# Normalised tiles handed to the next layer as two 16-bit planes in DRAM and turned by transposing DMAs

## The chip, the cores and the metric

The kernel runs on one core of one Trainium2 chip. The metric is the device time of one execution in microseconds. A core has TensorE (PE in the profile, with its weight loads as PEld), VectorE (DVE), ScalarE (ACT), GpSimd (POOL) and SyncE (SP). SP issues the DMAs here, in program order, and 16 DMA engines carry them out.

## The reference

A sequence of 2048 tokens with 1024 features goes through four layers in float32. Each layer projects its input to several streams, mixes them by its own recurrences, attentions and gates, and projects the result back to 1024 features. Cut to the frame that the change touches:

```python
x = first_block(x, ...)     # layer 1: gated recurrence + sliding-window attention
x = second_block(x, ...)    # layer 2 (even) and layer 3 (odd), same frame
return third_block(x, ...)  # layer 4: y = rms_norm(x, norm_g); x + out_proj(...)

# the frame of layers 1 to 3
h = jnp.einsum('btd,de->bte', x, w_in)          # input projection, 1024 -> several thousand
mix = ...                                       # recurrences, attention, gates
out = jnp.einsum('bte,ed->btd', mix, w_out)     # output projection, 1024 -> 1024
z = ALPHA * x + out
x = (z - mean(z)) * rsqrt(var(z) + 1e-5) * ln_g + ln_b
```

So the normalised rows of one layer are needed twice by the next: with features on partitions, as the input of the projection, and with tokens on partitions, as the residual. Layer 4 needs them scaled by `norm_g` per feature.

## The kernel before, in words

**Tiling.** The tokens are cut into four blocks of 512 (`TB`). A step is one layer on one block. `run` takes the blocks in pairs and the layers within a pair: (layer 1, block 0), (1, 1), (2, 0), (2, 1), and so on to layer 4, then blocks 2 and 3. There are 16 steps. What a step leaves is used by the next layer two steps later.

**Matrix products.** Every product of the two projections is done in three: the input is split into `ah` (rounded to the fast 32-bit form) and `al` (what rounding lost), the weights into `hi` and `lo`, and TensorE adds `hi*ah`, `hi*al` and `lo*ah` in one PSUM bank. `ah` and `al` are single tiles of 128 features x 8 chunks x 512 tokens. `out_proj` uses the same two tiles for the mixed streams, so the next step's input can be written into them only piece by piece, as the last products of the step before have read them.

**Weights.** A weight piece is 1 MB in a tile of the pool `whl` with four buffers. On first use it is fetched, split by ACT (L458) and DVE (L315), and saved to DRAM (`wdr`); afterwards it is loaded whole by one DMA on SP (L452). SP waits until TensorE has left a buffer before it can issue the next piece.

**End of a step.** `out_proj` multiplies in two halves of 512 output columns. In the second half it takes tokens 0 to 255 first and tokens 256 to 511 after them, and normalises each tile of 128 tokens as it comes out: tiles 1 and 3 get scale and shift (`lng`, `lnb`) on DVE at once, tiles 0 and 2 are only centred and scaled by their deviation on ACT. What remains is put into `pending` as four calls of `tail`, one for a tile of 128 tokens, and for layer 3 a fifth, `rms_row`.

**`tail`.** It turns a tile of 128 tokens x 1024 features by eight transposes on TensorE (`tr`, L327, each 128x128) into two PSUM banks. ACT copies them out to two tiles of the pool `t`: for tiles 0 and 2 in pieces of 128 with the scale and shift per feature (L707), for tiles 1 and 3 in one copy (L699), in layer 3 with the scale `ng`. Two DMAs (L708) write them to `chn` in DRAM, which then holds the features on partitions. For tiles 0 and 2 DVE then applies scale and shift to the rows, and one DMA (L714) writes the rows to `rows`.

**Start of a step.** All layers begin with `in_b4`: four groups of 128 output columns, each with its own weight piece and PSUM bank, first over tokens 0 to 255 (24 matmuls of 128x256 a group), then over tokens 256 to 511. After the first three groups of the first pass, and after the first two of the second, `flush` takes one call from `pending`. The `tail` of the step before thus runs inside the first products of the next.

**`load_x`.** For a new step it calls `load_x1` eight times, for each tile of 128 tokens and each half of the features: one DMA of 256 KB from `chn` (for layer 1 from the input `xt`, which lies in DRAM already turned) to a tile of the pool `u`, ACT's cast to `ah` (L587) and DVE's subtraction to `al`.

**Order.** The order of the instructions on each engine, and of the DMAs on SP, comes from a planner that runs when the kernel is built. It goes by the order in which the program states them, by tile buffers that come free and by priorities (`hp` for weights and some evictions). On the chip each engine keeps its order and waits on semaphores. Pools bound how far it runs ahead: 13 buffers of `u`, 7 of `t`, 4 of `whl`; four of `u` hold `lng` and `lnb` until the last `tail`.

Of the kernel before, what the change touches and what calls it, by code (L numbers as in the profile page):

```python
# [10 lines left out]
F32 = mybir.dt.float32  # L11
F32R = mybir.dt.float32r
I32 = mybir.dt.int32
U8 = mybir.dt.uint8
BF16 = mybir.dt.bfloat16
AF = mybir.ActivationFunctionType
ALU = mybir.AluOpType
# [3 lines left out]
D = 1024  # L21
T = 2048
TB = 512
# [203 lines left out]
class Build:  # L227
# [114 lines left out]
    def setup(self):  # L342
        nc = self.nc
# [14 lines left out]
        nc.gpsimd.affine_select(out=cm, in_=ones[:, 0:128], compare_op=ALU.is_ge, fill=0.0, base=0, pattern=[[1, 128]], channel_multiplier=-1)  # L358
        self.cmask = self.const([128, 128], U8, "cmask")
        nc.vector.tensor_copy(self.cmask, cm)  # L360
# [3 lines left out]
        nc.gpsimd.affine_select(out=self.amask, in_=zero, compare_op=ALU.is_ge, fill=NEGB, base=0, pattern=[[1, 128]], channel_multiplier=-1)  # L364
        self.rst = self.const([128, 512], BF16, "rst")
        nc.vector.memset(self.rst, 1.0)
# [10 lines left out]
        self.chn, self.rows = {}, {}  # L377
        for l in self.layers[:-1]:
            for i in range(2):
                self.chn[l, i] = self.dp.tile([4, 128, D], F32, tag=f"chn{l}{i}", name="chn")  # L380
                self.rows[l, i] = self.dp.tile([4, 128, D], F32, tag=f"rows{l}{i}", name="rows")

        lb = self.const([128, 4], F32, "lb")
# [15 lines left out]
        for n in ("hgw", "glag", "retg", "pscale", "mlg"):  # L399
            h = self.const([128, 4], F32, n + "h")  # L400
# [155 lines left out]

    def load_x(self, b, l):
        if not self.start:
            for t in range(4):
                for i in range(2):  # L560
                    self.load_x1(b, l, t, i)
            return

        ws = []
        self.wi, self.wpos = "wi1", 0
        for parts in (((0, 0), (1, 0)), ((0, 1), (1, 1)), ((2, 0), (3, 0)), ((2, 1), (3, 1))):
            for t, i in parts:
                with self.hp():
                    self.load_x1(b, l, t, i)
            ws.append(self.next_w())  # L570
        self.ahead, self.start = ws, False
        self.lc = self.lconst(l, b)
        with self.later(300):
            self.save()
# [5 lines left out]
    def load_x1(self, b, l, t, i):  # L580
        nc = self.nc
        st = self.u()
        src = self.I["xt"][b] if l == 1 else self.chn[l - 1, b % 2]
        self.first(nc.sync.dma_start(st, src[t, :, i * 512:i * 512 + 512]))
        c = slice(t * 128, t * 128 + 128)
        h = self.ah[:, 4 * i:4 * i + 4, c]
        nc.scalar.copy(h, c4(st))  # L587
        self.tt(self.al[:, 4 * i:4 * i + 4, c], c4(st), h.bitcast(F32), ALU.subtract)

    def load_xr(self, b, l):  # L590
        self.xr = self.big(self.at, [128, 4, D], F32)
        src = self.I["xr"][b] if l == 1 else self.rows[l - 1, b % 2]
        for t in range(4):
            self.tc.keep_in_program_order(self.nc.sync.dma_start(self.xr[:, t], src[t]))
# [93 lines left out]
    def tail(self, layer, b, xr, t, lng, lnb):  # L688

        nc = self.nc  # L690
        x = xr[:, t]
        for j in range(2):
            ps = self.mm()
            for i in range(4):
                k = 4 * j + i
                self.tr(ps[:, i * 128:i * 128 + 128], x[:, k * 128:k * 128 + 128])
            f = self.t()
            if t % 2 and layer < 3:
                nc.scalar.copy(f, ps)  # L699
            else:  # L700
                for i in range(4):
                    o = slice(i * 128, i * 128 + 128)
                    if t % 2:
                        self.act(f[:, o], ps[:, o], AF.Copy, scale=self.col("ng", 4 * j + i))
                    else:
                        k = 8 * (layer - 1) + 4 * j + i
                        self.act(f[:, o], ps[:, o], AF.Identity, scale=self.lgn[:, k:k + 1], bias=self.lbn[:, k:k + 1])  # L707
            nc.sync.dma_start(self.chn[layer, b % 2][t, :, j * 512:j * 512 + 512], f)  # L708
        if t % 2 == 0:
            for i in range(2):  # L710
                xi = x[:, i * 512:i * 512 + 512]
                self.tt(xi, xi, lng[i], ALU.mult)
                self.tt(xi, xi, lnb[i], ALU.add)
        nc.sync.dma_start(self.rows[layer, b % 2][t], x)  # L714

    def rms_row(self, b, xr):
# [1096 lines left out]
def c4(ap):  # L1813
    return ap.rearrange("p (a b) -> p a b", a=4)
# [22 lines left out]
```

## Time and profile before

| | |
|---|---|
| time, median of 3 runs | 3685.34 us (3682.23 to 3688.99) |
| the profiled execution | 3691.55 us, span 3689.8 us |
| TensorE busy | 3652.1 us (99%) in 20576 matmuls |
| VectorE busy | 2256.2 us (61%) |
| ScalarE busy | 1389.5 us (38%) |
| GpSimd busy | 14.9 us |
| DMA | 798.03 MB, 60.6% of 16 engines' span |
| granted TensorE clock | 0.999 |
| DMAs from `chn` (L584) | 96 of 256 KB, median 7.0 us to landing |
| DMAs to `chn` (L708) | 96 of 256 KB, median 3.5 us to landing |

Busy times are those of the records, and records of neighbouring matmuls overlap: the busy time of a group is what it adds to the engine's cover, the mean is the length of one record. In a row of groups the columns are line, engine, operation, what is written from what is read, shapes and count, then busy us and mean ns, then the idle time before it and who ended that. In a timeline row they are start, length, engine, line, operation, tiles and count.

### The profile page before, as it was taken

The numbers are of one execution on the slowest core, as the hardware profiler recorded it, in microseconds if no ns is written. First come the engines' busy times: TensorE is split into PE (matmuls) and PEld (weight loads), VectorE is DVE, ScalarE is ACT, GpSimd is POOL, SyncE is SP. The second block draws the span as 40 slices with busy tenths as digits, with TensorE's granted clock in tenths as the row PEclk, the third lists the DMA queues.
The fourth block names the chain that finished last, engine by engine and source line by source line (L and its number), as shares of the span: only waits on it lengthen the run. The fifth ranks groups of instructions, "written<-read, shape, count | busy, mean of one in ns | idle before, by whom it ended". The sixth has DMA issues, their size and how long they took to land.

```text
span 3689.8 us, 53341 instructions
## 1 busy us (share of the span) xinstructions
PE 3652.1 (99%) x20576; PEld 3090.4 (84%) x20576; DVE 2256.2 (61%) x5796; ACT 1389.5 (38%) x2890; POOL 14.9 (0%) x37
## 2 busy tenths in 40 slices
PE   8999999999999999999999999999999999999999
PEld 7888888888787888888888888989887878888887
DVE  7765566555755598587556556444454546883874
ACT  6636343323341355235254372313121313541451
POOL 0000000000000000000000000000000000000000
PEclk9999999999999999999999999999999999999999
DMA  7784577856885784853644645657475747446534
GB/s 274 252 291 156 199 266 278 296 182 231 308 305 202 249 288 166 296 189 104 215 180 167 251 167 185 241 178 267 161 259 182 275 176 254 149 145 208 184 114 160
DMA packets 161823, 798.03 MB, mean 216 GB/s; under 512 B 17952, under 2 KB 18080, under 8 KB 93984
## 3 DMA queue, kind: packets, MB, share of 16 engines
q1 hardware_dynamic: 161568, 794.62, 60.6%
q8 instruction: 162, 2.65, 0.3%
q14 instruction: 93, 0.76, 0.1%
HBM read 593.02 MB, written 201.52 MB: 215 GB/s over the span
## 4 chain that ended last, share of the span: by engine, by line
PE 60%; DVE 3%; ACT 1%; issue 0%; DMA 0%; SPq 0%; POOL 0%; POOLq 0%; DVEq 0%; ACTq 0%
PE acc L324 50%; PE mm L324 7%; PE mm L327 3%; DVE u L312 1%; DVE t L315 0%; DVE whl L315 0%; DVE big L312 0%; ACT t L302 0%; ACT u L301 0%; ACT t L301 0%; DMA wst<-in_wi_dram 0%; ACT whl L458 0%; DVE ss L1437 0%; ACT big L301 0%; DMA chn<-t 0%
## 5 line engine op out<-in xcount | busy, mean ns | idle before, releaser
L324 PE MATMUL acc<-whl,ah 128*128 128x512 f32 (+3 forms) x6144 | 1815.2, 379 | 2.8 <-DVE mix L312 1.9
L324 PEld LDWEIGHTS acc<-whl,ah 128*128 128x128 f32 x6144 | 1111.7, 188 | 226.2 <-issue 4.8
L324 PE MATMUL acc<-whl,al 128*128 128x512 f32 (+3 forms) x3072 | 1159.0, 377 | 0.0
L324 PE MATMUL acc<-ah,whl 128*128 128x256 f32 (+1 forms) x4096 | 1062.4, 343 | 9.1 <-ACT whl L458 8.3
L324 PEld LDWEIGHTS acc<-ah,whl 128*128 128x128 f32 x4096 | 699.4, 189 | 92.2 <-ACT whl L458 8.5
L324 PE MATMUL acc<-al,whl 128*128 128x512 f32 (+1 forms) x2048 | 697.1, 340 | 0.0
L324 PEld LDWEIGHTS acc<-whl,al 128*128 128x128 f32 x3072 | 578.2, 188 | 114.4
L324 PEld LDWEIGHTS acc<-al,whl 128*128 128x128 f32 x2048 | 386.7, 189 | 40.0 <-issue 3.6
L315 DVE TENSOR_TENSOR whl<-wst,whl 128x1024 fp32r<-128x1024 f32 (+3 forms) x141 | 167.0, 1185 | 112.2 <-ACT whl L458 109.6
L458 ACT CAST whl<-wst 128x1024 fp32r<-128x1024 f32 (+3 forms) x141 | 143.4, 1019 | 169.2 <-PE acc L324 102.2
L587 ACT CAST ah<-u 128x512 fp32r<-128x512 f32 x128 | 78.4, 620 | 271.5 <-PE acc L324 249.2
L312 DVE SCALAR_TENSOR_TENSOR big<-big,acc 128x512 f32<-128x512 f32 x128 | 86.3, 680 | 134.9 <-PE acc L324 134.6
L312 DVE SCALAR_TENSOR_TENSOR u<-mix,hdw,u 128x512 f32<-128x512 f32 x240 | 166.2, 741 | 0.3
L312 DVE SCALAR_TENSOR_TENSOR g<-g,acc 128x512 f32<-128x512 f32 x80 | 55.0, 687 | 162.3 <-ACT g L301 162.0
L301 ACT ACTIVATE g<-acc 128x512 f32<-128x512 f32 x72 | 42.9, 597 | 236.6 <-PE acc L324 236.5
L315 DVE TENSOR_TENSOR al<-u,ah 128x512 fp32r<-128x512 f32 x128 | 86.7, 680 | 51.5 <-ACT ah L587 51.4
L301 ACT ACTIVATE t<-mm,cols 128x128 f32<-128x128 f32 (+2 forms) x272 | 98.3, 462 | 51.2 <-PE mm L327 48.5
L324 PE MATMUL mm<-big,u 128*128 128x256 f32 (+2 forms) x616 | 92.4, 285 | 1.3 <-DVE u L315 1.3
L324 PEld LDWEIGHTS mm<-big,u 128*128 128x128 f32 x616 | 83.8, 189 | 6.7 <-DVE u L315 1.5
L1020 DVE CUSTOM_DVE_ANT_0 t<-mm,lc,nsk 128x256 f32<-128x256 f32 (+1 forms) x128 | 55.0, 472 | 49.4 <-PE mm L324 49.1
L324 PEld LDWEIGHTS mm<-vb,t 128*128 128x128 f32 (+1 forms) x640 | 67.9, 169 | 16.1 <-issue 9.5
L324 PE MATMUL mm<-vb,t 128*64 128x128 f32 (+2 forms) x640 | 78.8, 278 | 1.6 <-DVE t L312 0.9
(338 smaller groups left out, 4062.3 us busy)
## 6 DMA issues: line engine op xcount, KB each, us to landing
whl<-wdr SPq DMA_DIRECT2D x396, 1024.0 KB, 4.8
wdr<-whl SPq DMA_DIRECT2D x132, 1024.0 KB, 4.9
wst<-in_wi_dram SPq DMA_DIRECT2D x99, 512.0 KB, 6.2
rows<-big SPq DMA_DIRECT2D x48, 512.0 KB, 4.7
chn<-t SPq DMA_DIRECT2D x96, 256.0 KB, 3.5
u<-chn SPq DMA_DIRECT2D x96, 256.0 KB, 7.0
big<-rows SPq DMA_DIRECT2D x48, 512.0 KB, 7.0
wst<-in_wo_dram SPq DMA_DIRECT2D x32, 512.0 KB, 5.7
```

The source lines that it names most:

```text
L301: return self.nc.scalar.activation(out, in_, f, bias=bias, scale=scale)
L312: return self.nc.vector.scalar_tensor_tensor(out, in0, s, in1, op0, op1)
L315: return (eng or self.nc.vector).tensor_tensor(out, a, b, op)
L324: return self.nc.tensor.matmul(out, lhsT, rhs, start=start, stop=stop)
L327: return self.nc.tensor.transpose(out, in_, self.ident)
L458: nc.scalar.copy(hi[:, c], st[:, c])
L587: nc.scalar.copy(h, c4(st))
L1020: nc.vector.tensor_tensor_reduce(out=p[:, o + off:o + 256], in0=ps[:, o + off:o + 256], in1=band[:, off:256], scale=-0.125, scalar=self.ns ...
```

## The change

`chn` becomes two planes of 16-bit words, one with the low and one with the high half of each 32-bit number, and it holds tokens in rows, not features. `tail` no longer transposes. It brings tiles 0 and 2 to their final rows first, as before on DVE, then copies the two halves apart, the low one on DVE and the high one on ACT, each into a `t` tile of 128 x 1024 words, and writes each with one DMA.

`load_x` now calls `load_x2` eight times, for each half of the tokens (256) and each pair of feature chunks. It takes a `u` tile and a `t` tile, issues four transposing DMAs on SP (two planes, two chunks, each 256 tokens x 128 features of 16 bits), and puts the halves back together in the `u` tile: the high half by ACT, the low half by DVE. Then follow the cast to `ah` and the subtraction to `al`, for layer 4 chunk by chunk with the scale `ng`, which `tail` and the constants applied before. For layer 1 it loads the 32-bit input with two plain DMAs of 128 KB in place of one of 256 KB. The first load of the kernel still goes through `load_x1`, and `rows` stays as it is.

```diff
@@ -12,6 +12,7 @@
 F32R = mybir.dt.float32r
 I32 = mybir.dt.int32
 U8 = mybir.dt.uint8
+U16 = mybir.dt.uint16
 BF16 = mybir.dt.bfloat16
 AF = mybir.ActivationFunctionType
 ALU = mybir.AluOpType
@@ -377,7 +378,7 @@
         self.chn, self.rows = {}, {}
         for l in self.layers[:-1]:
             for i in range(2):
-                self.chn[l, i] = self.dp.tile([4, 128, D], F32, tag=f"chn{l}{i}", name="chn")
+                self.chn[l, i] = self.dp.tile([2, TB, D], U16, tag=f"chn{l}{i}", name="chn")
                 self.rows[l, i] = self.dp.tile([4, 128, D], F32, tag=f"rows{l}{i}", name="rows")
 
         lb = self.const([128, 4], F32, "lb")
@@ -556,9 +557,9 @@
 
     def load_x(self, b, l):
         if not self.start:
-            for t in range(4):
-                for i in range(2):
-                    self.load_x1(b, l, t, i)
+            for c in range(0, TB, 256):
+                for k in range(0, 8, 2):
+                    self.load_x2(b, l, slice(c, c + 256), k)
             return
 
         ws = []
@@ -580,12 +581,38 @@
     def load_x1(self, b, l, t, i):
         nc = self.nc
         st = self.u()
-        src = self.I["xt"][b] if l == 1 else self.chn[l - 1, b % 2]
-        self.first(nc.sync.dma_start(st, src[t, :, i * 512:i * 512 + 512]))
+        self.first(nc.sync.dma_start(st, self.I["xt"][b, t, :, i * 512:i * 512 + 512]))
         c = slice(t * 128, t * 128 + 128)
         h = self.ah[:, 4 * i:4 * i + 4, c]
         nc.scalar.copy(h, c4(st))
         self.tt(self.al[:, 4 * i:4 * i + 4, c], c4(st), h.bitcast(F32), ALU.subtract)
+
+    def load_x2(self, b, l, c, k0):
+
+        nc = self.nc
+        st = self.u((128, 2, 256))
+        if l == 1:
+            for t in range(2):
+                t1 = c.start // 128 + t
+                nc.sync.dma_start(st[:, :, t * 128:t * 128 + 128], self.I["xt"][b, t1, :, k0 * 128:k0 * 128 + 256].rearrange("p (k t) -> p k t", k=2))
+        else:
+            pl = self.t((128, 2, 2, 256), U16)
+            sv = st.bitcast(U16).rearrange("p k (t w) -> p k t w", w=2)
+            for w in range(2):
+                for k in range(2):
+                    nc.sync.dma_start_transpose(pl[:, w, k], self.chn[l - 1, b % 2][w, c, (k0 + k) * 128:(k0 + k) * 128 + 128])
+            nc.scalar.copy(sv[:, :, :, 1], pl[:, 1])
+            nc.vector.tensor_copy(sv[:, :, :, 0], pl[:, 0])
+        h, r = self.ah[:, k0:k0 + 2, c], self.al[:, k0:k0 + 2, c]
+        if l < 4:
+            nc.scalar.copy(h, st)
+            self.tt(r, st, h.bitcast(F32), ALU.subtract)
+            return
+
+        for k in range(2):
+            ng = self.col("ng", k0 + k)
+            self.act(h[:, k], st[:, k], AF.Copy, scale=ng)
+            self.stt(r[:, k], st[:, k], ng, h[:, k].bitcast(F32), ALU.mult, ALU.subtract)
 
     def load_xr(self, b, l):
         self.xr = self.big(self.at, [128, 4, D], F32)
@@ -689,28 +716,16 @@
 
         nc = self.nc
         x = xr[:, t]
-        for j in range(2):
-            ps = self.mm()
-            for i in range(4):
-                k = 4 * j + i
-                self.tr(ps[:, i * 128:i * 128 + 128], x[:, k * 128:k * 128 + 128])
-            f = self.t()
-            if t % 2 and layer < 3:
-                nc.scalar.copy(f, ps)
-            else:
-                for i in range(4):
-                    o = slice(i * 128, i * 128 + 128)
-                    if t % 2:
-                        self.act(f[:, o], ps[:, o], AF.Copy, scale=self.col("ng", 4 * j + i))
-                    else:
-                        k = 8 * (layer - 1) + 4 * j + i
-                        self.act(f[:, o], ps[:, o], AF.Identity, scale=self.lgn[:, k:k + 1], bias=self.lbn[:, k:k + 1])
-            nc.sync.dma_start(self.chn[layer, b % 2][t, :, j * 512:j * 512 + 512], f)
         if t % 2 == 0:
             for i in range(2):
                 xi = x[:, i * 512:i * 512 + 512]
                 self.tt(xi, xi, lng[i], ALU.mult)
                 self.tt(xi, xi, lnb[i], ALU.add)
+        xv = x.bitcast(U16).rearrange("p (n w) -> p n w", w=2)
+        for w in range(2):
+            f = self.t((128, D), U16)
+            (nc.scalar.copy if w else nc.vector.tensor_copy)(f, xv[:, :, w])
+            nc.sync.dma_start(self.chn[layer, b % 2][w, t * 128:t * 128 + 128], f)
         nc.sync.dma_start(self.rows[layer, b % 2][t], x)
 
     def rms_row(self, b, xr):
```

## The prediction

> **What bounds the kernel now.** I read the page's engine shares and its chain first, then TensorE's waits, then the rows of the transposes that the change removes, and last the stretch around a change of layer, where the new loads must fit.
>
> ```profile
> span 3689.8 us, 53341 instructions
> PE 3652.1 (99%) x20576; PEld 3090.4 (84%) x20576; DVE 2256.2 (61%) x5796; ACT 1389.5 (38%) x2890; POOL 14.9 (0%) x37
> ...
> DMA packets 161823, 798.03 MB, mean 216 GB/s; under 512 B 17952, under 2 KB 18080, under 8 KB 93984
> q1 hardware_dynamic: 161568, 794.62, 60.6%
> ...
> PE 60%; DVE 3%; ACT 1%; issue 0%; DMA 0%; SPq 0%; POOL 0%; POOLq 0%; DVEq 0%; ACTq 0%
> ```
>
> Of the waits (us, times, longest), one of TensorE's and the first of SP's:
>
> ```profile
> PE mm L327 <- ACT big L301: 1.7, 3, 0.9
> ```
>
> ```profile
> SPq L452 <- PE acc L324: 2078.9, 395, 13.6
> ```
>
> TensorE is busy for all but 38 us of the span, and what can be followed of the chain is TensorE. So work taken from TensorE comes off the time, unless something new makes TensorE wait. SP's queue spends 2079 us waiting until TensorE gives a weight buffer free. SP has idle time, but it issues in order, and its next weight goes out only just after the buffer comes free. Whatever is put into that line stands ahead of weights.
>
> **What is removed.** `tail` turns four tiles of 128x1024 for each of 12 steps (layers 1 to 3, four blocks): 384 transposes, in 48 bursts of eight.
>
> ```profile
> L327 PE MATMUL mm<-ident,big 128*128 128x128 f32 x384 | 49.9, 273 | 1.7 <-ACT big L301 1.7
> ...
> 249.36 0.28 PE L324 MATMUL acc<-al,whl 128*128 128x256 f32 x1
> 249.48 0.28 PE L324 MATMUL acc<-ah,whl 128*128 128x256 f32 x1
> 249.60 1.03 PE L327 MATMUL mm<-ident,big 128*128 128x128 f32 x8
> 250.39 0.37 PE L324 MATMUL acc<-ah,whl 128*128 128x256 f32 x1
> 250.59 0.28 PE L324 MATMUL acc<-al,whl 128*128 128x256 f32 x1
> ```
>
> The mean of 273 ns is the length of one record; they overlap. The starts give the price: the burst starts at 249.60 and the next matmul at 250.39, 0.79 us for eight. That matmul then holds the engine 0.20 us (250.39 to 250.59), where its neighbours take 0.12 (249.36 to 249.48). A burst costs 0.79 + 0.08 = 0.87 us, and 48 of them 42 us. The bounds are 38 (48 x 0.79) and the row's 50 us busy time. With them go 1.7 us of waits for the normalised tile. The sum takes -44.
>
> **What else leaves and comes on ACT and DVE.**
>
> ```profile
> L301 ACT ACTIVATE t<-mm,cols 128x128 f32<-128x128 f32 x256 | 87.4, 448 | 48.5 <-PE mm L327 48.5
> L699 ACT COPY t<-mm 128x512 f32<-128x512 f32 x32 | 17.1, 590 | 7.3 <-PE mm L327 7.3
> L587 ACT CAST ah<-u 128x512 fp32r<-128x512 f32 x128 | 78.4, 620 | 271.5 <-PE acc L324 249.2 <-issue 10.5 <-DMA u<-chn 7.2
> L315 DVE TENSOR_TENSOR al<-u,ah 128x512 fp32r<-128x512 f32 x128 | 86.7, 680 | 51.5 <-ACT ah L587 51.4
> L458 ACT CAST whl<-wst 128x1024 fp32r<-128x1024 f32 x131 | 137.0, 1048 | 162.8 <-PE acc L324 102.2 <-DMA wst<-in_wi_dram 47.9 <-DMA wst<-in_wo_dram 5.1
> L315 DVE TENSOR_TENSOR whl<-wst,whl 128x1024 fp32r<-128x1024 f32 x131 | 159.8, 1222 | 93.9 <-ACT whl L458 93.3
> ```
>
> ACT loses the evictions, 87 + 17 = 104 us. It gains 48 copies of a 16-bit half of 128x1024, estimated at the 1048 ns of the cast of that size (50 us), and 96 half-word merges of 512 elements at 620 ns (60 us). DVE gains 48 copies at up to 1222 ns (59 us) and 96 merges at up to 680 (65 us). Whether 16-bit words go faster is not shown; half these prices is the lower end. In layer 4 the column scale moves into the load and splits each cast and subtraction in two: 32 pairs more, some 12 us on ACT and 5 on DVE, by the 448 and 620 ns rows. So ACT gains about 18 us and DVE some 130, up to 65% busy, all spread. What matters is the twelve places where this meets a deadline. The copies in `tail` have none before the planes are read, a whole step later. The merges are the ones to watch.
>
> **The loads.** Twelve loads change from eight DMAs of 256 KB into 32 transposing ones of 64 KB, 384 in place of 96, all on SP among the weights. Layer 1's loads for three blocks become 16 DMAs of 128 KB instead of 8. The writes stay 96 DMAs of 256 KB.
>
> Here is the change from layer 1 to 2 at 2321.4: SP's queue, TensorE's first matmul of the new layer, the engines in three stretches (columns: busy us of PE, PEld, DVE, ACT, POOL, then clock, DMA share, GB/s).
>
> ```profile
> 2281.60 2.07 SPq L584 DMA_DIRECT2D u<-chn  x3
> 2287.15 0.32 SPq L452 DMA_DIRECT2D whl<-wdr  x1
> 2287.52 2.89 SPq L584 DMA_DIRECT2D u<-chn  x4
> ...
> 2313.22 0.32 SPq L452 DMA_DIRECT2D whl<-wdr  x1
> ...
> 2321.43 0.28 PE L324 MATMUL acc<-ah,whl 128*128 128x256 f32 x1
> ...
> 2281.60:2299.20 17.60, 17.60 (x85) 14.43 (x85) 4.88 (x8) 2.53 (x4) 0.00 (x0) 1.00 0.90 318
> 2299.20:2313.00 13.80, 13.80 (x60) 11.10 (x60) 7.55 (x15) 2.49 (x4) 0.00 (x0) 1.00 0.21 78
> 2313.00:2332.00 19.00, 19.00 (x129) 17.33 (x128) 17.62 (x61) 8.62 (x16) 0.24 (x1) 1.00 0.91 328
> ...
> whl<-wdr SPq DMA_DIRECT2D x396, 1024.0 KB, 4.8
> ...
> L708 SPq DMA_DIRECT2D chn<-t x96: 319/320/1793, 251.8 to 3107.4; - x96
> L584 SPq DMA_DIRECT2D u<-chn x96: 358/450/2097, 445.9 to 3353.1; - x96
> ...
> DMA to landing us min/median/max: 2.0/5.7/8.4
> ```
>
> Planes are written from 251.8 and first read at 445.9, 194 us later. Layer 1's 24 extra DMAs at 0.45 us of issue are 11 us of SP time, hidden where SP waits anyway. The loads start at 2281.60. The new layer's first weight goes out at 2313.22, takes 4.8 us to land and is needed at 2321.43: it has 8.21 - 4.8 = 3.4 us to spare. In between the DMA engines are free for 10% of 17.6 us and 79% of 13.8 us, 12.7 us. The old loads' own 2 MB make room for 5.9 us more (798.03 MB in 60.6% of 3689.8 us is 357 GB/s). So the 32 transposing DMAs have about 18.6 us, 0.58 us each, before they push that weight, and 22 us, 0.69 each, before TensorE waits. If they held only SP (31.6 us less three weights of 0.32) and left the engines to the weights, they would have some 30 us plus the same 3.4, about 1.05 each.
>
> What one costs, no row here shows. The lower end is its bytes, 64 KB at 357 GB/s, 0.18 us. The upper end is that each waits for the one ahead to land, 2.0 us for the quickest DMA on these planes. I take 0.45 us, the median time that SP needs to issue one of the present loads, because a DMA of a quarter of the bytes is then paced by its issue. Then 32 x 0.45 = 14.4 us fits into 18.6, and the loads cost nothing at TensorE.
>
> Two sections of the Trainium skill differ on this price, and both are estimates beside that sum. "Advanced Engine Details and Errata", section X-Bar Transpose (TRN2), says that transposing DMAs are about as fast as ordinary ones, 350-400 GB/s; 64 KB would be under 0.19 us and the sum would stay. "VectorE: DVE Perf Modes", section The three transpose paths, gives 1309 ns for 128x128 of 16 bits by DMA against 390 ns on TensorE and sends such a transpose to TensorE; two of those per DMA, 32 DMAs, would be 84 us a load, and by that the kernel would be several hundred us slower. No row of before shows a transposing DMA; TensorE's 0.10 us here is well under that page's 390 ns, which may mean that the table holds latencies.
>
> The merges: between 2281.6 and 2299.2 ACT is busy only 2.5 us and DVE 4.9. Four merges of 0.65 us each side per half, taken when data lands, fit there. If a merge stands in ACT's order ahead of a cast or of `out_proj`'s own split and its data is late, the work behind it waits; I allow 0.7 us per load for that, 8 us in all, between 0 and the 3.5 us of the second rival.
>
> **The sum.** The profiled execution took 3691.55 us (span 3689.8), 6.2 over the median of 3685.34. 3691.55 - 44 + 8 = 3656, and against the median 3649.
>
> **Rivals.**
>
> *Loads that choke the queue (slower).* Each transposing DMA costs more than 0.69 us, weights queue behind them on SP and on the engines, and TensorE waits at the twelve changes of layer for 32 x (c - 0.69) us each. At c = 0.80 this is 12 x 3.5 = 42 us and eats the gain; at 1.2, midway between 0.45 and 2.0, it is 12 x 16.3 = 196 and the time 3685 - 44 + 196 = 3837; at 2.0 it is 503 and the time 4144. For it: the DMA engines are 90% and 91% busy in two of the three stretches, weights have 3.4 us to spare, and four times as many DMAs carry the same bytes in short pieces. Against it: SP is idle most of the time, and the present loads issue at 0.45 us.
>
> *Late data in ACT's and DVE's line (same).* Casts and splits of the old layer stand behind merges that wait for their DMAs, or DVE, busy 17.6 of 19 us after 2313, hands the second half of the input over late. At 3.5 us a load the gain is gone: 3685. For it: in the row of L587 above ACT already waits 7.2 us for two loads. Against it: the second half is needed only after four groups of 24 matmuls of 0.12 us, 11 us later.
>
> *The shared tiles.* The merged tile takes one of seven `t` buffers until both merges are done, so an eighth transpose holds SP. It ends in the second rival's price or less.
>
> **Chances.** The forecast, all transposing DMAs within their window: 58%, 3634 (50 us gain, no stall) to 3675. Late data eating it: 10%. Choked queue: 32%, half of it beyond c = 1.2, where the VectorE page's table of the Trainium skill would put it. 0.2% (7 us) is about what a measurement can tell. The range goes from 3634 to 3840, to the 1.2 us case; the forecast's own is 3634 to 3675. Faster 58%, same 10%, slower 32%.
>
> **What would show it.** Right: no L327 row with `big` as input, TensorE's instructions down by 384, 384 DMA_TRANSPOSE-like rows on SP at about half a microsecond, TensorE's waits still under 40 us, DVE some 100 us busier, ACT about level. Wrong: transposing rows of 0.8 us and more, weights landing late, and TensorE idle before the first `acc<-ah,whl` of a layer or inside the second half of `out_proj`, released by a DMA or by a cast.

## The result: 3.3% slower

The changed kernel takes 3807.74 us (median of 4 runs, 3803.49 to 3811.90) against 3686.58 for the kernel before on the same chip: a ratio of 1.033, 95% interval 1.0312 to 1.0348. The forecast was 3649. The profiled execution after took 3806.18 us.

The page after, and TensorE's longest waits (us, times, longest):

```profile
span 3804.4 us, 53070 instructions
PE 3644.3 (96%) x20192; PEld 3066.4 (81%) x20192; DVE 2323.0 (61%) x5972; ACT 1409.4 (37%) x2778; POOL 14.4 (0%) x37
...
q1 hardware_dynamic: 267936, 794.66, 60.2%
...
PE 31%; DVE 3%; SPq 2%; DMA 1%; ACT 1%; issue 0%; POOL 0%; POOLq 0%; DVEq 0%; ACTq 0%
```

```profile
PE acc L325 <- DMA whl<-wdr: 94.7, 13, 23.7
PE acc L325 <- ACT ah L302: 17.2, 4, 6.0
PE acc L325 <- DVE g L313: 9.0, 3, 6.9
PE acc L325 <- ACT whl L459: 8.0, 3, 7.2
```

The transposes have left TensorE (20192 matmuls, 384 fewer), yet its busy time fell by only 8 us and its idle time grew from 38 to 160. Three quarters of the new idle time is weights that land late; that wait is not in the list of before. SP's queue, at 0% in the followed chain before, now has 2% of it. The DMA engines' share of the span is about that of before (60.2% after 60.6%, of a span 3% longer), which speaks against a lack of bandwidth on the whole. The rows of the new DMAs point elsewhere (durations in ns, shortest, median and longest; then first and last start):

```profile
L603 SPq DMA_TRANSPOSE t<-chn x384: 1102/1240/2707, 415.2 to 3460.1; - x192
...
DMA to landing us min/median/max: 2.2/2.5/14.9
```

SP needs 1.24 us to issue one transposing DMA, where it needs 0.32 for a weight of 1 MB. Here is SP's queue ahead of a change of layer, and TensorE's idle times in the same stretch:

```profile
2301.02 10.19 SPq L453 DMA_DIRECT2D whl<-wdr  x2
2311.30 27.49 SPq L603 DMA_TRANSPOSE t<-chn  x21
2338.89 0.52 SPq L453 DMA_DIRECT2D whl<-wdr  x1
2339.47 8.81 SPq L603 DMA_TRANSPOSE t<-chn  x7
2348.38 1.00 SPq L453 DMA_DIRECT2D whl<-wdr  x2
...
2352.16 7.08 SPq L603 DMA_TRANSPOSE t<-chn  x4
```

```profile
2344.17 1.20 PE L325 MATMUL acc<-whl,ah 128*128 128x512 f32 x2 [6.45 <-DMA whl<-wdr]
...
2353.48 0.70 PE L325 MATMUL acc<-whl,ah 128*128 128x512 f32 x2 [0.35 <-DMA whl<-wdr]
...
2365.75 1.22 PE L325 MATMUL acc<-whl,ah 128*128 128x512 f32 x2 [5.56 <-ACT ah L302]
```

21 transposing DMAs hold SP for 27.49 us, in which no weight goes out. TensorE has used up the pieces it had by 2337.7; the weight of 2338.89 comes too late, and it stands for 6.45 us. The second long wait, at 2365.75, has another releaser: `out_proj`'s split on ACT. The row of ACT before it shows why.

```profile
2352.49 2.66 ACT L604 COPY u<-t 128x512 uint16<-128x512 uint16 x4
2364.39 0.76 ACT L604 COPY u<-t 128x512 uint16<-128x512 uint16 x1 [9.24 <-DMA t<-chn]
2365.02 1.25 ACT L302 ACTIVATE ah<-mm,hgwh 128x512 fp32r<-128x512 f32 x2
```

ACT waited 9.24 us for a transposed piece whose merge stands in its order ahead of the split that TensorE needed. That is the second rival of the prediction. The four DMAs of this piece are the last of SP's rows above: they went out only from 2352.16 on.

A standstill costs more than its own length. In this table of the same stretch a row ends with the granted clock, the DMA engines' busy share and GB/s:

```profile
2300.00:2339.00 39.00, 37.72 (x209) 31.48 (x207) 22.31 (x64) 11.40 (x37) 0.00 (x0) 1.00 0.31 89
2339.00:2344.00 5.00, 0.00 (x0) 0.00 (x0) 0.00 (x0) 0.00 (x0) 0.00 (x0) 0.83 0.81 254
2344.00:2348.00 4.00, 3.83 (x9) 3.12 (x10) 0.00 (x0) 0.00 (x0) 0.00 (x0) 0.50 0.29 58
2348.00:2364.00 16.00, 11.84 (x56) 9.14 (x55) 2.65 (x6) 3.81 (x6) 0.00 (x0) 0.93 1.00 300
2364.00:2371.00 7.00, 5.25 (x15) 4.12 (x16) 1.67 (x3) 1.88 (x3) 0.00 (x0) 0.60 0.62 262
```

After standing still TensorE runs at half clock from 2344 to 2348, and a pair of matmuls takes 1.20 us. At full clock such a pair takes about 0.63. The table also shows that bandwidth is not plentiful at every moment: from 2348 to 2364 the DMA engines are full (1.00), with three weights and four loads of constants that went out between 2348.38 and 2351.61. The late piece had to land among them, so that may have a part in ACT's wait.

### The profile page after: what moved, and what is told of

It is laid out like the page before. It is cut to its first block, busy times and chain, and to the rows that moved or that the text cites. A ratio compares the mean times of both kernels' runs of the same rounds, so it can differ in the third digit from the quotient of the medians.

```text
span 3804.4 us, 53070 instructions
## 1 busy us (share of the span) xinstructions
PE 3644.3 (96%) x20192; PEld 3066.4 (81%) x20192; DVE 2323.0 (61%) x5972; ACT 1409.4 (37%) x2778; POOL 14.4 (0%) x37
## 3 DMA queue, kind: packets, MB, share of 16 engines
q1 hardware_dynamic: 267936, 794.66, 60.2%
## 5 line engine op out<-in xcount | busy, mean ns | idle before, releaser
L608 ACT CAST ah<-u 128x512 fp32r<-128x512 f32 x88 | 54.5, 620 | 214.7 <-PE acc L325 147.4
L604 ACT COPY u<-t 128x512 uint16<-128x512 uint16 x96 | 66.2, 771 | 89.9 <-DMA t<-chn 80.4
L316 DVE TENSOR_TENSOR al<-u,ah 128x512 fp32r<-128x512 f32 x96 | 64.9, 678 | 52.7 <-ACT ah L608 51.4
L727 ACT COPY t<-big 128x1024 uint16<-128x1024 uint16 x48 | 49.1, 1046 | 86.3 <-DVE vy L313 44.6
```

The costliest lines, as they stand in the source:

```text
L316: return (eng or self.nc.vector).tensor_tensor(out, a, b, op)
L604: nc.scalar.copy(sv[:, :, :, 1], pl[:, 1])
L608: nc.scalar.copy(h, st)
L727: (nc.scalar.copy if w else nc.vector.tensor_copy)(f, xv[:, :, w])
```

## The experiments

The theory: the price is SP's time to issue a transposing DMA, fixed per instruction; weights stand behind it (A). Rivals: the transposing DMAs hold the DMA engines (B), or the larger number of DMAs and the merges cost the time whatever the DMAs are (C). The short diffs are against the changed kernel unless said; in them `src` and `chn` stand for the slice and the planes that the changed kernel reads. The ratio is to the kernel before on the same chip, with its 95% interval.

**Ordinary DMAs in place of the transposing ones.** The words come in unturned, so this run shows the time alone.

```diff
-nc.sync.dma_start_transpose(pl[:, w, k], src)
+nc.sync.dma_start(pl[:, w, k].rearrange("p (a c) -> p a c", a=2), src.rearrange("(a p) c -> p a c", a=2))
```

> Every transposing DMA is replaced by an ordinary DMA of the same 64 KB, the same 256-byte source rows, the same count (384) and the same place; the next layer then reads words that are not turned. Theory A (SP needs 1.24 us to issue one transposing DMA, and weights stand behind it): issue falls to about 0.4 us each, TensorE's wait for whl falls from 95 to under 15 us, its idle time is under 60 us, the time 3640 to 3665. Rival C (the four times larger number of DMAs and the merges on ACT and DVE cost the time, whatever kind of DMA): above 3750.

3653.47 us, ratio 0.9904 (0.9887 to 0.9921).

```profile
span 3652.0 us, 53055 instructions
PE 3614.4 (99%) x20192; PEld 3054.2 (84%) x20192; DVE 2323.4 (64%) x5972; ACT 1410.6 (39%) x2778; POOL 14.6 (0%) x37
...
L603 SPq DMA_DIRECT2D t<-chn x384: 359/467/2047, 415.7 to 3313.7; - x192
```

The loss goes when the DMAs don't transpose, with as many DMAs and the same merges; C falls. TensorE's busy time is 37.7 us below before, and its idle time is 38 us as before. So the removed transposes are worth nearly what the prediction gave them, the merges and copies cost nothing that can be seen, and 384 issues at 0.47 us in place of 96 at 0.45 are hidden. The DMA engines are busy as long as in the changed kernel: 62.6% of 3652.0 us are 2286, 60.2% of 3804.4 are 2290. Against this run the changed kernel has 122 us more idle time on TensorE and 30 us more busy time in the same 20192 matmuls. The clock is 0.998 here and 0.982 there.

But one thing more changed than the kind of DMA. The planner gave SP another order, so the expectation's "same place" does not hold: of the 96 groups of four DMAs, 55 stand elsewhere among SP's other DMAs. At the change of layer shown above, a weight goes out after 10 loads, not after 21:

```profile
2230.17 0.32 SPq L453 DMA_DIRECT2D whl<-wdr  x1
2230.58 5.99 SPq L603 DMA_DIRECT2D t<-chn  x10
2238.43 0.33 SPq L453 DMA_DIRECT2D whl<-wdr  x1
2238.81 4.87 SPq L603 DMA_DIRECT2D t<-chn  x8
```

This run alone does not separate the price of an issue from the order. The next one does.

**The same bytes in half as many transposing DMAs.**

```diff
-for k in range(2):
-    nc.sync.dma_start_transpose(pl[:, w, k], chn[w, c, (k0 + k) * 128:(k0 + k) * 128 + 128])
+nc.sync.dma_start_transpose(pl[:, w], chn[w, c, k0 * 128:k0 * 128 + 256])
```

> One transposing DMA takes both feature chunks of a plane (256 tokens x 256 features, 128 KB): 192 in place of 384, the same bytes. If the price is one per instruction: 1.2 to 1.5 us each, SP holds 230 to 290 us in them in place of 476, the time 3680 to 3720. If the price goes by the 16x128 pieces turned: about 2.4 us each, SP time unchanged, the time 3790 to 3820.

3659.70 us, ratio 0.9922 (0.9907 to 0.9937): faster than before, and faster than either branch had expected.

```profile
L602 SPq DMA_TRANSPOSE t<-chn x192: 1187/1258/2804, 413.5 to 3307.0; - x192
...
PE acc L325 <- DMA whl<-wdr: 5.9, 1, 5.9
```

Twice the bytes cost 1.26 us in place of 1.24. In this run SP's order is exactly that of the changed kernel, with one DMA where two stood. At the same change of layer 11 DMAs hold SP where 21 did, for 14.79 us in place of 27.49, and TensorE is busy all through (15.00 of 15.00 us in the last row, which is one of the table of stretches):

```profile
2221.77 10.19 SPq L453 DMA_DIRECT2D whl<-wdr  x2
2232.05 14.79 SPq L602 DMA_TRANSPOSE t<-chn  x11
2246.94 0.52 SPq L453 DMA_DIRECT2D whl<-wdr  x1
...
2232.00:2247.00 15.00, 15.00 (x85) 12.89 (x84) 8.45 (x31) 3.55 (x19) 0.00 (x0) 1.00 0.63 159
```

The price is one per instruction, and at 16 DMAs a load SP has room for them.

**Half of the transposing DMAs, each as large as in the changed kernel.** Only the high plane is transposed, the low one goes by ordinary DMAs.

```diff
-nc.sync.dma_start_transpose(pl[:, w, k], src)
+if w: nc.sync.dma_start_transpose(pl[:, w, k], src)
+else: nc.sync.dma_start(...)   # as in the run with ordinary DMAs
```

> Only the high plane goes by transposing DMAs (192 of the same size), the low plane by ordinary ones; its words are not turned. Theory A: SP holds 192 x 1.24 + 192 x 0.4 = 315 us in the loads, the time lies between the one with ordinary DMAs alone and the changed kernel, 3690 to 3740, and under the middle of the two because short rows of transposes fit into the weights' lead. Rival C: above 3750, as with all kinds.

3666.27 us, ratio 0.9938 (0.9923 to 0.9953), better than A's figures: the cost does not grow in proportion to the number of transposes. But here too the planner moved 28 of the 96 groups, and a weight goes out after 13 loads at the change shown, not after 21. How much of the miss is the order is not shown.

**Quarter-size and four-chunk DMAs.** First 128 tokens x 128 features (768 DMAs of 32 KB), then 256 tokens x 512 features (96 of 256 KB, one plane's four chunks in one `t` tile).

```diff
+for t in range(2):   # 32 KB each
+    nc.sync.dma_start_transpose(pl[:, w, k, t * 128:t * 128 + 128], chn[w, r, (k0 + k) * 128:(k0 + k) * 128 + 128])
```

```diff
+p = self.t((128, 4, 256), U16)   # 256 KB, for k0 = 0 and 4
+nc.sync.dma_start_transpose(p, chn[w, c, k0 * 128:k0 * 128 + 512])
```

> The same planes turned in 768 transposing DMAs of 128 tokens x 128 features (32 KB). Theory A with a price per instruction: 1.1 to 1.25 us each, 64 x 1.2 = 77 us of SP per load, about 27 us of which fit, the time 4150 to 4350. If the price goes by the pieces turned: 0.6 us each, the time near the changed kernel's, 3790 to 3830.

> One transposing DMA takes four feature chunks of a plane (256 tokens x 512 features, 256 KB): 96 of them, as many DMAs as before. If the price stays one per instruction: about 1.3 us each, 125 us of SP in all, the time that of ordinary DMAs, 3645 to 3660. If the data begins to pace it: 2 us and more each, the time above that with two chunks, 3660 to 3690.

4248.53 us (one run) and 3649.50 us, ratio 0.9898 (0.9881 to 0.9914), both within the range for a price per instruction. SP's order is again that of the changed kernel. The issue rows, of the small ones and then of the large ones:

```profile
L605 SPq DMA_TRANSPOSE t<-chn x768: 1093/1230/2592, 414.2 to 3903.8; - x192
```

```profile
L596 SPq DMA_TRANSPOSE t<-chn x96: 1237/1297/5189, 414.0 to 3300.4; - x96
```

1.23 us for 32 KB, 1.24 for 64, 1.26 for 128, 1.30 for 256: over a factor of eight in bytes the price moves by 5%. Setting SP's time in the loads (DMAs per load x median) against the change of time gives this table:

| version | SP us per load | time against before | SP's order |
|---|---|---|---|
| 8 transposing of 256 KB | 8 x 1.30 = 10 | -36 | as changed |
| 32 ordinary of 64 KB | 32 x 0.47 = 15 | -34 | another |
| 16 transposing of 128 KB | 16 x 1.26 = 20 | -28 | as changed |
| 16 transposing, 16 ordinary | 27 | -21 | another |
| 32 transposing of 64 KB | 32 x 1.24 = 40 | +121 | as changed |
| 64 transposing of 32 KB | 64 x 1.23 = 79 | +563 | as changed |

In the changed kernel's order, up to 20 us per load is hidden but for 8 us in all. From 40 to 79 us, 39 us more in each of 12 loads, the time grows by 442 us: 0.94 us for each of SP's. The edge lies between 20 and 40.

**The weights on another queue,** and the control for that step in the kernel before.

```diff
-nc.sync.dma_start(w.bitcast(F32), kept)
+nc.gpsimd.dma_start(w.bitcast(F32), kept)
```

> The 420 loads of stored weights go out on POOL's queue; the transposing DMAs stay on SP. Theory A (the weights are late because they stand behind transposing DMAs in SP's line): TensorE's wait for whl falls under 20 us, the waits for ACT's split of the mix remain, the time 3670 to 3720. Rival B (the transposing DMAs hold the DMA engines, so that weights are late from any queue): the wait for whl stays above 70 us and the time above 3770.

> The kernel before, with the loads of stored weights on POOL's queue: the control for the same step in the changed kernel. If POOL's queue serves the weights as well as SP's, the time stays within 0.5% of before (3670 to 3705), and what the changed kernel kept above before with its weights on POOL (52 us) belongs to the late data of the loads themselves. If POOL's queue is the cost, this run loses 30 us or more as well.

3740.19 us, ratio 1.0143 (1.0128 to 1.0158), worse than A expected, and 3696.01 us for the control, ratio 1.0024 (1.0014 to 1.0033). TensorE's waits in the first:

```profile
PE acc L325 <- ACT ah L302: 33.8, 9, 10.9
PE acc L325 <- DVE big L313: 12.7, 2, 12.5
PE acc L325 <- DMA whl<-wdr: 9.7, 11, 1.8
```

The wait for weights falls from 95 to 10 us: from another queue they are nearly on time while the same transposing DMAs run. B falls with that, and SP's queue is shown to be what held them. But the time comes down by only 67 of 154 us (3808 against 3653 with ordinary DMAs). The transposed data itself is still late: ACT waits 101.8 us for it, against 80.4 in the changed kernel, and TensorE's wait for ACT's split of the mix grows from 17.2 to 33.8. POOL's queue cost the kernel before 10 us. The planner changed the order here too; how the 87 us that are left divide among these is not shown.

**The transposing DMAs on ACT's queue.**

```diff
-nc.sync.dma_start_transpose(...)
+nc.scalar.dma_start_transpose(...)
```

> The 384 transposing DMAs go out on ACT's queue; weights stay on SP. Theory A (the price is time of the queue that issues): weights are on time, the wait for whl is under 15 us, but ACT's evictions and splits stand behind 1.2 us issues and TensorE waits for ACT instead: 3700 to 3850. If the price came from SP alone: ACT issues them in under 0.5 us each and the time is 3650 to 3680.

3895.25 us (one run), above the expected range.

```profile
L603 ACTq DMA_TRANSPOSE t<-chn x384: 1117/1261/2877, 416.1 to 3548.0; - x192
...
PE acc L325 <- DVE g L313: 70.6, 5, 20.1
PE acc L325 <- ACT u L302: 62.9, 4, 22.0
PE mm L325 <- DVE mix L322: 28.6, 3, 11.0
PE mm L328 <- DVE mix L313: 25.2, 3, 19.0
```

ACT pays the same 1.26 us. TensorE's list has no wait for a stored weight any more, but ACT's evictions stand behind the issues (one row of 16 holds ACT for 22.40 us), and DVE behind them. SP's other DMAs keep their order. It is the time of whichever queue issues.

**The merges out of ACT's and DVE's lines.** The last question was whether the second wait, at ACT's split, is a cost of its own.

```diff
-nc.scalar.copy(sv[:, :, :, 1], pl[:, 1])
-nc.vector.tensor_copy(sv[:, :, :, 0], pl[:, 0])
+nc.gpsimd.tensor_copy(sv[:, :, :, 1], pl[:, 1])
+nc.gpsimd.tensor_copy(sv[:, :, :, 0], pl[:, 0])
```

> The changed kernel with both half-word merges on POOL, which is idle, so that neither ACT nor DVE waits in its line for the transposed data; SP's order is nearly the same. If the second price of late data (out_proj's split on ACT standing behind a merge) is real and separate, TensorE's wait for ACT's ah (17 us) falls under 5 us, the wait for whl stays at 80 us or more, and the time falls by 15 to 40 us to 3765 to 3795. If those waits only follow from the late weights, the time stays within 10 us of the changed kernel, 3798 to 3818.

3783.17 us, ratio 1.0264 (1.0247 to 1.0281), 25 us less than the changed kernel.

```profile
PE acc L325 <- DMA whl<-wdr: 94.0, 13, 22.9
PE acc L325 <- DVE g L313: 11.4, 3, 7.4
PE acc L325 <- ACT whl L459: 7.0, 1, 7.0
```

The wait for weights stays as it was, the 17 us at ACT's split are gone from the list, and SP's order is that of the changed kernel. So the second wait is separate: late data in an in-order line, worth about 25 us of the 154. The run also takes the merges' own work off ACT and DVE, but with ordinary DMAs that work cost nothing that could be seen.

## Why the prediction was wrong

**The failed step is one term: the price of a transposing DMA.** I took 0.45 us, the issue time of the present loads, between ends of 0.18 and 2.0. It measured 1.24. That a DMA of a quarter of the bytes is paced by its issue was right. But the issue is just what differs for a transposing DMA, and no row of ordinary DMAs could show it. At 0.47 us, with ordinary DMAs, the forecast of 3649 is met within 5 us. That closeness is in part luck: the bursts gave 37.7 us, not 42, and the 8 us allowed for late merges did not come (38 us idle, as before).

**The rival that came true** was the choked queue, at the price it named: 3837 at 1.2 us, and 3807.74 measured at 1.24. That its 1.2 us comes so near is in part luck. At the measured 1.24 its formula gives 12 x 32 x (1.24 - 0.69) = 211 us of waiting, against 154 of loss over the run with ordinary DMAs, because it let transposing DMAs hold the engines. They hold them no longer than ordinary ones (2290 us against 2286), and weights from another queue were nearly on time. With the prediction's other figure, 1.05 us for SP alone held, the same formula gives 73 us, too little. The prediction gave all 32 DMAs one window ahead of the new layer; the planner put them in rows of 21, 7 and 4 between weights at the change shown, and the first row already made TensorE wait. The table puts the edge between 20 and 40 us per load; the prediction's two figures were 22 and 34. Of the loss, 122 us are idle time of TensorE and 30 are the same matmuls taking longer at a lower clock, which the prediction did not count at all.

**Late data in ACT's line** was given as an alternative at 10%. It came together with the choked queue, as a part of it: 17 us of waits, about 25 us of time.

**What held.** TensorE's gain: 42 us forecast for the bursts, 37.7 us less busy time with ordinary DMAs. ACT's net: +18 forecast, +20 measured (1389.5 to 1409.4). DVE: +130 at the upper prices forecast, +67 at half of them and +67 measured, because its 16-bit copies are quick (0.69 us for 1024 words, 0.45 for 512); ACT's were 1.05 and 0.77, the second above the 0.62 I took. None of these decides anything. The shared `t` tiles did not show as a bound.

**The two sections of the Trainium skill.** "Advanced Engine Details and Errata", section X-Bar Transpose (TRN2), calls transposing DMAs as fast as ordinary ones. For their bytes the four-chunk run agrees: its 256 KB take a median of 5.4 us from issue to landing, where the ordinary loads of 256 KB before took 7.0. For the time of the queue it does not hold here: 1.24 us against 0.47. "VectorE: DVE Perf Modes", section The three transpose paths, gives 1309 ns for one 128x128 of 16 bits by DMA. The 32 KB DMA of that shape took 1.23 us of its queue here, close to that figure. It is no price for larger ones: two such blocks in one DMA took 1.24, not 2.6. The rule that sends such a transpose to TensorE stands in the same page's section Rules for kernel authors; here, with TensorE at 99%, the kernel with DMAs of 256 KB was 1.0% faster than the one with TensorE's transposes. On the clock, "TensorE: Matmul & The Clock Gate", section Part 1: The HAM clock gate, says that an idle window of about 3.4 us halves the clock and a busy one of that length restores it. The trace agrees: after 6.45 us of waiting, half clock from 2344 to 2348, and by 2349.30 a pair of matmuls takes 0.62 us again.

## What to carry to other kernels

Price a new kind of DMA by the time that its queue needs to issue it, and hold that against what stands behind it in that queue, in the order that the planner gives; the DMA engines' busy time over the span did not show it. A changed DMA can change that order too, so compare the order before reading a difference. Where the issue is a fixed price, make the DMA larger: four times the bytes in a quarter of the instructions turned 1.033 into 0.9898, with no change in buffers. Where the engine that bounds the kernel is at 99%, a stall also costs the slower clock behind it: 30 us on 122 here, and 64 on 531 with DMAs of 32 KB, whose stalls are longer (64.4 us the longest, 23.7 here).

## What the runs showed of the hardware

A transposing DMA of 16-bit words holds the queue that issues it for 1.23 to 1.30 us on SP, from 32 KB to 256 KB, and for 1.26 on ACT with 64 KB; an ordinary one of 64 KB in 256-byte rows takes 0.47. Short rows alone cost no time that could be seen: packets under 512 bytes went from 17952 to 121248 in the run with ordinary DMAs, and it gained 34 us.
